# Turning an expert's inner rows in two row halves of the array instead of all at once

## The chip, the cores and the metric

The kernel runs on one core of a Trainium2 chip. The metric is the device time of one execution in microseconds (us), here the median of 3 runs. Engines are named as the profile names them: PE is TensorE's matmul, PEld its load of the stationary operand (the weights of a matmul), DVE is VectorE, ACT ScalarE, POOL GpSimd, SP SyncE, whose queue issues the loads from HBM.

## The reference

A decoder trunk of two layers on 256 tokens of width 1024, all in float32. Layer 0 is attention (dilated windows and differential heads) and a dense SwiGLU. Layer 1 is a gated linear recurrence and then eight SwiGLU experts, of which each token takes its two best:

```python
logits = (t @ w_router).astype(F32)
top_vals, top_idx = lax.top_k(logits, TOP_K)
top_w = jax.nn.softmax(top_vals, axis=-1)
gates = jnp.sum(jax.nn.one_hot(top_idx, N_EXPERTS, dtype=F32) * top_w[..., None], axis=1)
out = jnp.zeros((B * S, D), F32)
for e in range(N_EXPERTS):
    y = swiglu(t, w_gate[e], w_up[e], w_down[e]).astype(F32)
    out = out + gates[:, e:e + 1] * y
```

`swiglu(u, w_gate, w_up, w_down)` is `(silu(u @ w_gate) * (u @ w_up)) @ w_down`, with an inner width of 3584 per expert. The change touches the product in the outer brackets, the expert's inner rows, on its way from the up projection to the down projection.

## The kernel before

Experts are taken in pairs. The tokens of an expert are gathered into 128 slots by matmuls with one-hot matrices (`gather_steps`, L1121), so that the slots are the columns of `xgh` and `xgl`, the high and the low part of the activations. Each expert's inner width is cut into 7 chunks of 512; one expert and one chunk is a `Job` (L1187), 56 in all.

A job has four pieces. `gate` and `up` multiply the slots by 512 columns of two weights and leave 128 slots x 512 inner columns in PSUM; `up` multiplies the two on DVE into `hm` (L1227), with the slots on the partitions. The down projection needs the inner columns on the partitions, so `turn` (L1231) transposes `hm` in four blocks of 128x128 by TensorE (L1235) into one PSUM bank, from which ACT copies the high part `hh` (L1239) and DVE subtracts it to give the low part `hl` (L1240). `down` multiplies them by 512 rows of the third weight.

Weights come as raw float32 tiles by SP's queue (L85), 14 of them in a ring. Each piece of 128x1024 elements, a split, is divided on ACT into a high part `w_hi` and on DVE into a low part `w_lo` (L91). A split is read by six matmuls of 512 columns: `mm3` (L100) multiplies high by high, high by low and low by high (L101 to L103), twice. Four splits are in flight, since `w_hi` and `w_lo` have four buffers each and `run` (L1168) makes a split ready three splits ahead of its use.

The order of the work of three engines is written out by hand. `in_turn` (L1113) issues a step behind the last step of PE, ACT and DVE that is in `tails`. `order` (L1342) puts the steps of neighbouring jobs between each other: the gate of a job, the turn of the job before, the up projection, the down of the job before. Where a pair of experts ends, the turn stands between two halves of the next gather, and the slots of the next pair follow (`slot_rows`, L1091). After the last job, turn and down follow each other directly.

PSUM has 8 banks: 4 with the tag `acc`, 2 with `pj` (the outputs of down), 2 with `tp`. `bank("tp")` (L75) hands out the two `tp` banks in rotation, to `turn` and to `slot_rows` among others.

Of the kernel before, what the change touches and what calls it, by code (L numbers as in the profile page):

```python
# [9 lines left out]
F32R = mybir.dt.float32r  # L10
I32 = mybir.dt.int32
U32 = mybir.dt.uint32
AF = mybir.ActivationFunctionType
# [3 lines left out]
P = 128  # L17
# [17 lines left out]
def f32(ap):  # L35
    return ap.bitcast(F32)
# [3 lines left out]
def tile_trunk(  # L40
# [22 lines left out]
    nc = tc.nc  # L63
# [11 lines left out]
    def bank(tag, bufs=2):  # L75
        return psum.tile([P, 512], F32, name=tag, tag=tag, bufs=bufs)
# [135 lines left out]
    ident = const.tile([P, P], F32, name="ident")  # L212
# [90 lines left out]
    def norm_T(hgs, gain, acc, into=None):  # L303

        xh, xl = into or x_tiles()
        rs = []
        for t in range(NT):
            for c in range(2):
                nc.vector.tensor_add(h[t][:, HALF[c]], acc[t][c], h[t][:, HALF[c]])
                nc.vector.tensor_mul(hgs[t][:, HALF[c]], h[t][:, HALF[c]], gain[:, HALF[c]])  # L310
            r, pw = rms(t)
            rs.append(r)
            for c in range(2):
                to_T(hgs[t], xh, xl, t, 4 * c, 4 * c + 4)
        return xh, xl, rs, pw
# [45 lines left out]
    with tc.tile_pool(name="att", bufs=2) as att, tc.tile_pool(name="atc", bufs=1) as atc:  # L361
# [19 lines left out]
        for t in range(NT):  # L381
            r = atc.tile([P, 2], F32, name=f"r2{t}")
# [41 lines left out]
        class Group:  # L424
# [49 lines left out]
            def turn(self):  # L474
                self.qT = att.tile([P, 2, S], F32, name="qT", tag="qT", bufs=1)
                self.kT = att.tile([P, 2, S], F32, name="kT", tag="kT", bufs=1)
                gq, gk = (cols[:, 2:3], cols[:, 3:4]) if self.g == 3 else (cols[:, 0:1], cols[:, 1:2])
                for t in range(NT):
                    pt = bank("tp")
                    for i in range(4):  # L480
                        nc.tensor.transpose(out=pt[:, i * P:(i + 1) * P], in_=self.qk[t][:, i * P:(i + 1) * P], identity=ident)
                    ptv = pt.rearrange("p (a b) -> p a b", b=P)
                    nc.scalar.activation(self.qT[:, :, TOK[t]], ptv[:, 0:2], AF.Copy, scale=gq)
                    nc.vector.tensor_scalar(self.kT[:, :, TOK[t]], ptv[:, 2:4], gk, None, op0=ALU.mult)
# [227 lines left out]
    with tc.tile_pool(name="hga", bufs=2) as hga, tc.tile_pool(name="hg", bufs=2) as hg, tc.tile_pool(name="hgc", bufs=1) as hgc:  # L712
        C = 64
# [261 lines left out]
    moe = ctx.enter_context(tc.tile_pool(name="moe", bufs=2))  # L975
# [9 lines left out]
    _, _, rx, pw = norm_T(hg_, gain_m, acc, into=dense)  # L985
# [125 lines left out]
    tails = {}  # L1111

    @contextmanager  # L1113
    def in_turn():

        with ExitStack() as st:
            for i in tails.values():
                st.enter_context(tc.issue_after(i.ins))
            yield
# [67 lines left out]
    class Job:  # L1187
# [41 lines left out]
            return self.into(self.wu) + [out_]  # L1229

        def turn(self):  # L1231
            pt = bank("tp")
            with in_turn():
                for i in range(4):
                    tails["pe"] = nc.tensor.transpose(out=pt[:, i * P:(i + 1) * P], in_=self.hm[:, i * P:(i + 1) * P], identity=ident)  # L1235
                self.hh = moe.tile([P, 4, P], F32R, name="hh", tag="hh", bufs=1)
                self.hl = moe.tile([P, 4, P], F32R, name="hl", tag="hl", bufs=1)
                ptv = pt.rearrange("p (a b) -> p a b", b=P)
                tails["act"] = nc.scalar.activation(self.hh, ptv, AF.Copy)  # L1239
                tails["dve"] = nc.vector.tensor_sub(self.hl, ptv, f32(self.hh))  # L1240

        def down(self):
            sh, ch = self.shared, self.ch
# [145 lines left out]
    with tc.If(most > P):  # L1389
        ecur = mc.tile([P, 1], F32, name="ecur")  # L1390
        nc.vector.memset(ecur, 0.0)
        with tc.For_i(0, NE, 1) as e:
# [16 lines left out]
            for src, dst in ((nh, xg2[0]), (nl, xg2[1])):  # L1409
                for k0 in range(0, KT, 4):  # L1410
                    pt = bank("tp")
# [54 lines left out]
```

## Time and profile before

| | |
|---|---|
| median of 3 runs | 1479.27 us (1476.80 to 1481.37) |
| the profiled execution | 1475.87 us, of it a span of 1474.2 us from the first to the last instruction |
| mean granted TensorE clock over the span | 0.996 of full speed |
| busy PE, PEld, DVE, ACT | 1439.5, 1220.1, 1231.7 and 1059.0 us |
| the stretch of the experts | from about 500 us to the end |

Matmuls are pipelined: one starts before the one ahead of it has ended, so a busy time of PE is no measure of how well the array is used. The pace of PE is read from the distance between starts. PEld overlaps PE: the load of the next matmul's weights usually runs under the stream of the one before.

### The profile page before, as it was taken

Reading aid. Unit: us, or ns where it says so; the run is one execution under the profiler, and the core shown is the slowest. Engines: PE = TensorE matmul, PEld = TensorE weight load, DVE = VectorE, ACT = ScalarE, POOL = GpSimd, SP = SyncE. Lnnn points to the kernel's source line nnn. Section 1 sums busy time; section 2 is a strip of 40 time slices with the busy share of each in tenths; the row PEclk is TensorE's granted clock in tenths of the full one; section 3 lists DMA queues with packets and bytes.
Section 4 is the critical chain, followed back from the end, with each engine's and each line's share of the span. In section 5 each row is a group of like instructions: output and inputs, shape, how many; then the busy total and the mean of one; then the engine's idle time right before and its main releaser. Section 6 shows DMA issues by size and latency. Waiting matters only on the chain.

```text
span 1474.2 us, 20073 instructions
## 1 busy us (share of the span) xinstructions
PE 1439.5 (98%) x7509; PEld 1220.1 (83%) x7509; DVE 1231.7 (84%) x1460; ACT 1059.0 (72%) x1285; POOL 32.5 (2%) x45
## 2 busy tenths in 40 slices
PE   7999999999999999999999999999999999999996
PEld 6887899998889788888888888888888888888885
DVE  7776656556867899999999999989999999999995
ACT  6655544445756688888888888888888888888884
POOL 1000000000000100000000000000000000000000
PEclk9999999999999999999999999999999999999998
DMA  9933355656443399999999999999999999999971
GB/s 315 369 131 115 129 189 183 184 188 186 137 165 135 137 349 378 376 375 383 371 345 378 375 369 384 392 337 384 370 376 366 394 378 344 380 370 372 384 266 16
DMA packets 209692, 434.05 MB, mean 294 GB/s; under 512 B 7403, under 2 KB 58643, under 8 KB 209587
## 3 DMA queue, kind: packets, MB, share of 16 engines
q1 hardware_dynamic: 207506, 425.77, 79.8%
q0 software_dynamic: 2080, 6.92, 2.1%
q8 instruction: 61, 1.00, 0.3%
q14 instruction: 45, 0.36, 0.1%
HBM read 427.41 MB, written 5.24 MB: 293 GB/s over the span
## 4 chain that ended last, share of the span: by engine, by line
issue 61%; PE 29%; DMA 5%; DVE 2%; ACT 2%; POOL 0%; SPq 0%; POOLq 0%; ACTq 0%; DVEq 0%
DMA out_dram<-y,idx 4%; PE acc L101 3%; PE acc L102 3%; PE acc L103 3%; PE pj L342 3%; PE pj L344 3%; PE pj L343 3%; PE pj L101 1%; PE pj L103 1%; PE pj L102 1%; PE pj L760 1%; PE pj L761 1%; PE pj L762 1%; DVE w_lo L91 1%; PE tp L556 1%
## 5 line engine op out<-in xcount | busy, mean ns | idle before, releaser
L91 DVE TENSOR_TENSOR w_lo<-raw,w_hi 128x1024 fp32r<-128x1024 f32 x810 | 975.1, 1223 | 156.6 <-ACT w_hi L91 116.9
L91 ACT ACTIVATE w_hi<-raw 128x1024 fp32r<-128x1024 f32 x810 | 853.5, 1062 | 299.7 <-PE acc L103 127.5
L101 PE MATMUL acc<-w_hi,xgh 128*128 128x512 f32 x904 | 357.2, 395 | 0.9 <-ACT xgh L294 0.9
L103 PE MATMUL acc<-w_hi,xgl 128*128 128x512 f32 x904 | 352.7, 390 | 0.0
L102 PE MATMUL acc<-w_lo,xgh 128*128 128x512 f32 x904 | 352.4, 390 | 0.0
L103 PEld LDWEIGHTS acc<-w_hi,xgl 128*128 128x128 f32 x904 | 169.7, 188 | 36.1
L101 PEld LDWEIGHTS acc<-w_hi,xgh 128*128 128x128 f32 x904 | 169.8, 188 | 34.9 <-ACT xgh L294 1.2
L102 PEld LDWEIGHTS acc<-w_lo,xgh 128*128 128x128 f32 x904 | 169.9, 188 | 33.6
L103 PE MATMUL pj<-w_hi,hl 128*128 128x512 f32 x448 | 174.5, 389 | 0.0
L102 PE MATMUL pj<-w_lo,hh 128*128 128x512 f32 x448 | 174.3, 389 | 0.0
L101 PE MATMUL pj<-w_hi,hh 128*128 128x512 f32 x448 | 163.5, 390 | 0.7 <-ACT hh L1239 0.7
L101 PEld LDWEIGHTS pj<-w_hi,hh 128*128 128x128 f32 x448 | 84.1, 188 | 18.2 <-ACT hh L1239 0.9
L103 PEld LDWEIGHTS pj<-w_hi,hl 128*128 128x128 f32 x448 | 84.1, 188 | 17.9 <-DVE hl L1240 0.4
L102 PEld LDWEIGHTS pj<-w_lo,hh 128*128 128x128 f32 x448 | 84.1, 188 | 17.4
L342 PE MATMUL pj<-xh,w_hi 128*128 128x256 f32 x320 | 90.8, 284 | 0.6 <-DVE hm L677 0.6
L344 PE MATMUL pj<-xh,w_lo 128*128 128x256 f32 x320 | 90.6, 283 | 0.0
L343 PE MATMUL pj<-xl,w_hi 128*128 128x256 f32 x320 | 90.6, 283 | 0.0
L342 PEld LDWEIGHTS pj<-xh,w_hi 128*128 128x128 f32 x320 | 61.4, 192 | 1.2 <-DVE hm L677 0.8
L343 PEld LDWEIGHTS pj<-xl,w_hi 128*128 128x128 f32 x320 | 61.4, 192 | 0.4
L344 PEld LDWEIGHTS pj<-xh,w_lo 128*128 128x128 f32 x320 | 61.4, 192 | 0.0
L101 PE MATMUL acc<-w_hi,xh 128*128 128x512 f32 (+1 forms) x160 | 58.7, 368 | 1.5 <-ACT xh L294 0.8
L102 PE MATMUL acc<-w_lo,xh 128*128 128x512 f32 (+1 forms) x160 | 57.6, 361 | 0.0
(300 smaller groups left out, 1538.5 us busy)
## 6 DMA issues: line engine op xcount, KB each, us to landing
raw<-in_moe_w_gate_dram SPq DMA_DIRECT2D x112, 1024.0 KB, 7.5
raw<-in_moe_w_up_dram SPq DMA_DIRECT2D x112, 1024.0 KB, 7.7
raw<-in_moe_w_down_dram SPq DMA_DIRECT2D x110, 1024.0 KB, 7.3
raw<-in_ffn_w_gate_dram SPq DMA_DIRECT2D x22, 512.0 KB, 3.7
raw<-in_ffn_w_up_dram SPq DMA_DIRECT2D x22, 512.0 KB, 4.8
raw<-in_ffn_w_down_dram SPq DMA_DIRECT2D x11, 1024.0 KB, 4.9
raw<-in_hgrn_w_in_dram SPq DMA_DIRECT2D x10, 1024.0 KB, 5.6
raw<-in_attn_w_in_dram SPq DMA_DIRECT2D x16, 512.0 KB, 8.9
```

The lines of the kernel that those rows point to most:

```text
L91: split.last = nc.scalar.activation(hi, view, AF.Copy), nc.vector.tensor_sub(lo, view, f32(hi))
L101: nc.tensor.matmul(ps, lhsT=xh, rhs=wh, start=first, stop=False, skip_group_check=chk)
L102: nc.tensor.matmul(ps, lhsT=xh, rhs=wl, start=False, stop=False, skip_group_check=chk)
L103: return nc.tensor.matmul(ps, lhsT=xl, rhs=wh, start=False, stop=last, skip_group_check=chk)
L342: nc.tensor.matmul(o, lhsT=wh[:, i, j], rhs=xh[:, k], start=k == 0 and j == 0, stop=False, skip_group_check=True)
L343: nc.tensor.matmul(o, lhsT=wh[:, i, j], rhs=xl[:, k], start=False, stop=False, skip_group_check=True)
L344: nc.tensor.matmul(o, lhsT=wl[:, i, j], rhs=xh[:, k], start=False, stop=k == KT - 1, skip_group_check=True)
L556: nc.tensor.matmul(po[:, j * 64:(j + 1) * 64], lhsT=pT[:, kb, j, :], rhs=v[:, kb, j * 64:(j + 1) * 64], start=(j == 0 and kb == 0), stop=( ...
L760: nc.tensor.matmul(o, lhsT=wh[:, k], rhs=xh[:, k], start=first, stop=False, skip_group_check=True)
L761: nc.tensor.matmul(o, lhsT=wh[:, k], rhs=xl[:, k], start=False, stop=False, skip_group_check=True)
L762: nc.tensor.matmul(o, lhsT=wl[:, k], rhs=xh[:, k], start=False, stop=last, skip_group_check=True)
```

## The change

`turn` transposes the slots in two halves, partitions 0 to 63 and 64 to 127. Each of the four blocks becomes two transposes with 64 rows of `hm` as stationary operand and a 64x64 corner of the identity as moving operand, in alternation between the halves. The first half's results go into one `tp` bank and the second half's into the other, 256 columns each. ACT and DVE make `hh` and `hl` from the two banks in two instructions each. C is 64.

```diff
         def turn(self):
-            pt = bank("tp")
+            pts = [bank("tp") for _ in range(2)]
+            self.hh = moe.tile([P, 4, P], F32R, name="hh", tag="hh", bufs=1)
+            self.hl = moe.tile([P, 4, P], F32R, name="hl", tag="hl", bufs=1)
+            parts = [slice(r * C, (r + 1) * C) for r in range(2)]
             with in_turn():
+
                 for i in range(4):
-                    tails["pe"] = nc.tensor.transpose(out=pt[:, i * P:(i + 1) * P], in_=self.hm[:, i * P:(i + 1) * P], identity=ident)
-                self.hh = moe.tile([P, 4, P], F32R, name="hh", tag="hh", bufs=1)
-                self.hl = moe.tile([P, 4, P], F32R, name="hl", tag="hl", bufs=1)
-                ptv = pt.rearrange("p (a b) -> p a b", b=P)
-                tails["act"] = nc.scalar.activation(self.hh, ptv, AF.Copy)
-                tails["dve"] = nc.vector.tensor_sub(self.hl, ptv, f32(self.hh))
+                    for rr, pt in zip(parts, pts):
+                        m = nc.tensor.transpose(out=pt[:, i * C:(i + 1) * C], in_=self.hm[rr, i * P:(i + 1) * P], identity=ident[rr, rr])
+                tails["pe"] = m
+                for rr, pt in zip(parts, pts):
+                    ptv = pt[:, 0:4 * C].rearrange("p (a b) -> p a b", b=C)
+                    a = nc.scalar.activation(self.hh[:, :, rr], ptv, AF.Copy)
+                    d = nc.vector.tensor_sub(self.hl[:, :, rr], ptv, f32(self.hh[:, :, rr]))
+                tails["act"], tails["dve"] = a, d
```

## Rows read from the trace of the kernel before

**Rows 1.** The page, busy us, share of the span and instructions of each engine.
```profile
PE 1439.5 (98%) x7509; PEld 1220.1 (83%) x7509; DVE 1231.7 (84%) x1460; ACT 1059.0 (72%) x1285; POOL 32.5 (2%) x45
```

**Rows 2.** Busy us per stretch: PE, PEld, DVE, ACT, POOL, then clock, DMA share, GB/s.
```profile
800.00:1100.00 300.00, 300.00 (x1374) 249.09 (x1373) 278.27 (x256) 243.78 (x254) 3.64 (x2) 1.00 1.01 374
```

**Rows 3.** Groups, 525 to 1456 us: count | busy us, mean ns | idle before, releasers.
```profile
L91 DVE TENSOR_TENSOR w_lo<-raw,w_hi 128x1024 fp32r<-128x1024 f32 x656 | 787.2, 1223 | 57.6 <-ACT w_hi L91 20.1
...
L1240 DVE TENSOR_TENSOR hl<-tp,hh 128x512 fp32r<-128x512 f32 x55 | 38.0, 692 | 9.2 <-ACT hh L1239 9.0
...
L1235 PE MATMUL tp<-ident,hm 128*128 128x128 f32 x218 | 32.7, 272 | 0.0
L1239 ACT ACTIVATE hh<-tp 128x512 fp32r<-128x512 f32 x55 | 32.6, 592 | 0.9 <-PE tp L1235 0.9
L1235 PEld LDWEIGHTS tp<-ident,hm 128*128 128x128 f32 x217 | 26.9, 140 | 6.7
```

**Rows 4.** Timeline around one turn: start us, us, engine, line, what, count.
```profile
915.12 0.40 PE L103 MATMUL acc<-w_hi,xgl 128*128 128x512 f32 x1
...
915.36 0.60 PE L1235 MATMUL tp<-ident,hm 128*128 128x128 f32 x4
...
915.80 0.19 PEld L102 LDWEIGHTS acc<-w_lo,xgh 128*128 128x128 f32 x1
```

**Rows 5.** Timeline, layer 0's attention scores, row halves alternating into two banks.
```profile
62.86 0.39 PE L103 MATMUL acc<-w_hi,xl 128*128 128x512 f32 x1
63.17 0.52 PEld L510 LDWEIGHTS pj<-kT,qT 64*128 64x128 f32 x8 [0.35 <-issue]
63.18 0.71 PE L510 MATMUL pj<-kT,qT 64*128 64x128 f32 x8
...
63.82 0.19 PEld L101 LDWEIGHTS acc<-w_hi,xh 128*128 128x128 f32 x1
...
63.93 0.19 PEld L102 LDWEIGHTS acc<-w_lo,xh 128*128 128x128 f32 x1
```

**Rows 6.** Timeline, layer 1's recurrence, matmuls on 64 rows of the array.
```profile
385.19 1.42 PEld L877 LDWEIGHTS tp<-v,kt 64*128 64x128 f32 x12
385.19 1.61 PE L877 MATMUL tp<-v,kt 64*128 64x128 f32 x12
...
386.73 0.19 PEld L760 LDWEIGHTS pj<-xh,w_hi 128*128 128x128 f32 x1
```

**Rows 7.** Timeline, the router's transposes of 8 rows.
```profile
497.00 0.39 PE L101 MATMUL acc<-w_hi,xgh 128*128 128x512 f32 x1
...
497.32 0.20 PEld L1036 LDWEIGHTS tp<-ident,lT 8*128 8x128 f32 x2 [0.36 <-DVE lT L1033]
```

**Rows 8.** Groups, 100 to 125 us: the same two copies at half the size.
```profile
L294 DVE TENSOR_TENSOR xl<-tp,xh 128x256 fp32r<-128x256 f32 x2 | 0.8, 416 | 0.0
...
L294 ACT ACTIVATE xh<-tp 128x256 fp32r<-128x256 f32 x2 | 0.8, 390 | 0.0
```

**Rows 9.** Timeline behind the turn of rows 4.
```profile
917.62 3.50 DVE L91 TENSOR_TENSOR w_lo<-raw,w_hi 128x1024 fp32r<-128x1024 f32 x3 [0.26 <-ACT w_hi L91]
...
919.91 0.19 PEld L102 LDWEIGHTS acc<-w_lo,xgh 128*128 128x128 f32 x1
```

**Rows 10.** Timeline of PE where a pair of experts ends.
```profile
979.03 0.60 PE L1235 MATMUL tp<-ident,hm 128*128 128x128 f32 x4
979.38 0.59 PE L1096 MATMUL tp<-info,oneh 128*128 128x4 f32 x4
```

**Rows 11.** Timeline, turn and down of the last job.
```profile
1456.16 0.60 PE L1235 MATMUL tp<-ident,hm 128*128 128x128 f32 x4
1456.79 0.60 ACT L1239 ACTIVATE hh<-tp 128x512 fp32r<-128x512 f32 x1 [0.74 <-PE tp L1235]
...
1457.44 0.19 PEld L101 LDWEIGHTS pj<-w_hi,hh 128*128 128x128 f32 x1 [0.92 <-ACT hh L1239]
...
1458.16 0.19 PEld L103 LDWEIGHTS pj<-w_hi,hl 128*128 128x128 f32 x1 [0.43 <-DVE hl L1240]
```

## The prediction

> **What bounds the kernel now.** The page's first part comes first: PE is busy for 98% of the span [rows 1]. Since matmuls overlap, that alone proves little. The stretches follow: in 300 us of the experts' part PE has no hole, the granted clock is 1.00 (the level of 2.4 GHz), DVE works 278 us and ACT 244 us, and HBM delivers 374 GB/s [rows 2]. The groups of the same part then say who waits: the idle time ahead of PE's transposes is 0.0, while DVE and ACT wait for each other and for PE [rows 3]. So PE sets the pace between 525 and 1456 us, and DVE is next with 93%. What the array does in a turn is worth its full length there; what ACT and DVE do is worth nothing until they are late.
>
> The timeline of one turn gives its price [rows 4]. The last matmul of the gate starts at 915.12. Four transposes start from 915.36 on; they take 0.60 us together and the last 0.27 [rows 3], which puts starts 0.11 us apart. The first matmul behind them begins to stream when the load of the one after it begins, at 915.80. From last matmul to next matmul: 0.68 us. Nothing is drained: the loads run under the streams ahead of them.
>
> **The change part by part.** The number of columns that stream stays: 4 transposes of 128 become 8 of 64. A gain needs two halves of the array to work at the same time, and the trace shows that they can. In layer 0, eight matmul instructions on 64 rows each, in alternation between the halves and into two banks, have their loads in 0.52 us [rows 5]; one takes 0.19, so first and last start 0.33 apart. That is three intervals of 0.11, so the eight went as four pairs. Twelve such loads that did not pair, in the recurrence, took 1.42 us, 0.11 apart each [rows 6].
>
> The same block shows what it costs to get in and out. The last full matmul starts at 62.86 and the first load on half the rows at 63.17: 0.31 us, where a successor in full rows starts after 0.23 (72 matmuls and a turn of 0.45 fill a job's 16.8 us). The 0.09 between is a drain, and the load behind it is covered by nothing. At the other end the last pair starts at 63.18 + 0.71 - 0.27 = 63.62, streams 0.11, and the next load is at 63.82: another 0.09. That load, too, is open, until 63.93. The recurrence has the same exit: 385.19 + 1.61 - 0.27 = 386.53 to 386.73, 0.20 [rows 6]. The router's transposes of 8 rows enter 0.32 after the start of the matmul ahead [rows 7].
>
> So the turn after the change, from the start of the gate's last matmul to the start of the next one:
>
> - to the first load: 0.31 [rows 5].
> - the first load, open: 0.06. A load for a transpose is shorter than for a matmul: 140 ns against 190 as recorded [rows 3, 5], and two of them with 8 rows took 0.20 together, so they start 0.06 apart [rows 7].
> - three intervals between four pairs: 64 columns at 0.11 per 128 make 0.055, the load 0.06; the longer one counts, 0.17 in all.
> - the last pair's start to the next load: 0.20 less the half of 0.11, as 64 columns stream and not 128: 0.15.
> - the next load, open: 0.11 [rows 5].
>
> The sum is 0.80 us against 0.68: 0.12 us more per turn. In words: pairing saves some 0.2 us of streaming, and two drains with two open loads cost 0.33.
>
> No row has transposes in alternating halves, so the bounds: at worst a block costs as much as that of rows 5, which streams twice the columns: 63.93 - 62.86 = 1.07, or 0.39 more per turn. At best pairs cost no drain: 0.68 - 0.22 = 0.46, or 0.22 less. I take 0.12, since entry, exit and pairing each have rows of their own, and only the halving of the width is worked out.
>
> The Trainium skill, "TensorE: Matmul & The Clock Gate", section "LDWEIGHTS (loading the stationary operand)", has a load take its columns divided by 1.2 GHz whatever the rows, here 107 ns. By that the first load and the three intervals would be 0.11 each, and the sum an estimated 1.01 us, 0.33 more per turn. The 0.06 between two loads of 128 columns speaks against it for transposes.
>
> ACT makes two copies of 390 ns in place of one of 592, DVE two of 416 in place of one of 692 [rows 3, 8]: 0.19 and 0.14 us more per turn. Queued behind them are the next `w_hi` on ACT and `w_lo` on DVE, and PE waits for that. The tightest place is the fourth split behind a turn: its `w_lo` starts at 917.62, ends 1.22 later at 918.84, and its first reader loads at 919.91 [rows 9]. Of 1.07 us some 0.33 go at most, and the reader is 0.12 later. Over a job DVE then works 12 x 1.223 + 0.83 + 0.69 = 16.2 us of 16.9 and still catches up. Price: nothing. If that cover were gone, 0.33 us per turn, 18 us in all.
>
> Two banks are now taken per turn, of two. The turn before is a job away, so `turn` itself waits for nothing. At the end of a pair of experts, though, `slot_rows` follows the transposes directly [rows 10] and needs the first of these banks, which is free once ACT and DVE have finished the first half, 0.39 + 0.42 us and some waiting later. Sixteen gather matmuls stand ready to go first. I take 0; three stalls of 1.1 us, 3 us, if not.
>
> In the last job nothing covers the turn: PE waits for `hh` and then for `hl` [rows 11]. There the drains run under a wait, and the halves let DVE start on the first while ACT copies the second: 0.39 + 2 x 0.42 = 1.23 us plus hand-overs against 0.59 + 0.69 = 1.28. I take 0 for this one.
>
> DMA issues are not moved. Sum: 55 turns x 0.12 = 6.6 us. On the profiled execution's own time, 1475.87, that makes 1482.5. This execution lies 3.4 us below the median of the three runs, 1479.27, and the forecast for a median is 1486 us, 0.45% slower. About 0.3%, 4.4 us, is what a measurement of this kernel can tell from no change.
>
> **The rivals.**
>
> *The halves do not pair.* The recurrence's matmuls on half rows alternate in the code and still ran one after the other [rows 6]; the order on the engine is not always the order in the code. Then eight intervals of 0.06 take the place of four: 0.31 + 0.06 + 7 x 0.06 + 0.15 + 0.11 = 1.05, so 0.37 more per turn, 20 us, 1499. The same comes out, near enough, if they pair but each load takes 0.11 (18 to 19 us), or if the copies eat the slack. Against it: both banks are free at every turn, so nothing reorders the halves.
>
> *Faster: full and half rows change over without a drain when both are transposes or the queue is full.* The place is the start of the first load after the gate: if it comes 0.01 after the array is free, as in the turn of before [rows 4], and not 0.09, and the loads hide, then 0.68 - 0.22 per turn, 55 x 0.22 = 12 us less, 1467. It decides from the point at which entry and exit together cost under 0.2 us. Against it stand the changes of rows in three parts of the trace [rows 5, 6, 7].
> The Trainium skill, "TensorEngine Tiling (Array Packing)", section "Theoretical Speedup", promises up to 2x for a small dimension of 64, which is this case; the same page names the drain on a change of mode but gives it no price.
>
> *No change that can be told.* If half of the open loads or drains hides, the turn costs under 0.08 us more, which is within 4.4 us. For it speaks that PE's queue is full here, whereas the blocks of rows 5 and 7 had waited for DVE or ACT shortly before.
>
> **How the numbers follow.** The forecast, 4 to 9 us slower, 0.62; no pairing, slow loads or late copies, 15 to 22 us slower, 0.20; no change, 0.12; faster, 0.06. Some of the forecast's own range lies at the bound, so slower has 0.80, same 0.14 and faster 0.06. The range reaches from the better end of the forecast, 1482, to the case without pairing, 1499; 1482 to 1489 is the likeliest case's own.
>
> **What would show it.** The transposes should come as pairs that start within 0.01 us, four starts 0.06 apart, in a block of 64-row instructions like that of rows 5. The gate's last matmul to the first load should be 0.31 us, the last pair to the next load 0.15, and the distance from one turn to the next 0.12 longer than the 16.8 of before. PE should still wait for nobody. The prediction is wrong if the first load comes less than 0.25 after the gate's last matmul, if eight starts stand apart, or if PE waits for `w_lo` or a bank.

## The result, and the profile after

The changed kernel takes 1485.6 us in the median, the kernel before 1476.8 in the runs beside it: a ratio of 1.0063, with a 95% interval of 1.0051 to 1.0075. It is slower by 9.3 us by the ratio and by 8.8 by the medians, and by more than 0.3%. One of its seven executions, at a granted clock of 0.805, took 1691.94 us and is left out of the ratio. The profiled execution has a span of 1483.8 us against 1474.2.

The page's first part and the stretch of rows 2, in the changed kernel; PE still has no hole, and clock and HBM are as before:

```profile
PE 1447.8 (98%) x7733; PEld 1212.3 (82%) x7733; DVE 1235.5 (83%) x1516; ACT 1062.0 (72%) x1341; POOL 32.5 (2%) x45
```
```profile
800.00:1100.00 300.00, 300.00 (x1436) 244.32 (x1435) 276.39 (x272) 242.86 (x272) 3.64 (x2) 1.00 1.00 370
```

The timeline of one turn, which answers to [rows 4]:

```profile
542.93 0.39 PE L103 MATMUL acc<-w_hi,xgl 128*128 128x512 f32 x1
...
543.25 0.33 PEld L1240 LDWEIGHTS tp<-ident,hm 64*128 64x128 f32 x8 [0.35 <-issue]
543.25 0.46 PE L1240 MATMUL tp<-ident,hm 64*128 64x64 f32 x8
...
543.64 0.19 PEld L101 LDWEIGHTS acc<-w_hi,xgh 128*128 128x128 f32 x1
...
543.75 0.19 PEld L102 LDWEIGHTS acc<-w_lo,xgh 128*128 128x128 f32 x1
543.85 0.66 ACT L1244 ACTIVATE hh<-tp 128x256 fp32r<-128x256 f32 x2
...
544.26 0.76 DVE L1245 TENSOR_TENSOR hl<-tp,hh 128x256 fp32r<-128x256 f32 x2
```

From the gate's last matmul to the first matmul behind the turn: 543.75 - 542.93 = 0.82 us, where it was 0.68. The first load comes 0.32 after that matmul. Eight loads take 0.33 together; one takes 0.14 (below), so the first and the last start 0.19 apart, in three steps of 0.06. A window that ends behind the second pair shows the pairs: four loads in 0.20, which is one step of 0.06 and one load of 0.14.

```profile
543.25 0.20 PEld L1240 LDWEIGHTS tp<-ident,hm 64*128 64x128 f32 x4 [0.35 <-issue]
```

The groups from 526.5 to 1463 us (count | busy us, mean ns | idle us before), which answer to [rows 3]:

```profile
L91 DVE TENSOR_TENSOR w_lo<-raw,w_hi 128x1024 fp32r<-128x1024 f32 x654 | 787.8, 1224 | 70.9 <-ACT w_hi L91 31.5
...
L1245 DVE TENSOR_TENSOR hl<-tp,hh 128x256 fp32r<-128x256 f32 x110 | 41.6, 420 | 0.3
...
L1244 ACT ACTIVATE hh<-tp 128x256 fp32r<-128x256 f32 x110 | 36.1, 385 | 0.8 <-PE tp L1240 0.8
...
L1240 PE MATMUL tp<-ident,hm 64*128 64x64 f32 x440 | 25.4, 235 | 0.0
L1240 PEld LDWEIGHTS tp<-ident,hm 64*128 64x128 f32 x436 | 17.7, 137 | 18.4 <-issue 18.0
```

The last line shows the way in: PEld has 18.4 us of idle time ahead of the transposes' loads, put down to "issue", the name for time in which nothing that the profile shows is waited for. In the kernel before it was 6.7 [rows 3]. The 11.7 between them is not itself the loss, which was 8.1 and is read from the distances below. The transposes' union of busy time went the other way, from 32.7 us to 25.4: the pairs do save. A reader who ranks lines by busy time would take the change for a gain.

The turns are now 16.95 us apart, by 0.15 more than before, and 55 x 0.147 (0.817 - 0.670, before rounding) makes 8.1 us; from the first turn to the last it took 939.77 us, and 931.56 before. The spans differ by 9.6; most of the rest came ahead of any changed instruction, for the first turn starts at 526.30 in this execution and at 524.59 in the one of before.

### The profile page after: what moved, and what is told of

It is laid out like the page before. It is cut to its first block, busy times and chain, and to the rows that moved or that the text cites. A ratio compares the mean times of both kernels' runs of the same rounds, so it can differ in the third digit from the quotient of the medians.

```text
span 1483.8 us, 20633 instructions
## 1 busy us (share of the span) xinstructions
PE 1447.8 (98%) x7733; PEld 1212.3 (82%) x7733; DVE 1235.5 (83%) x1516; ACT 1062.0 (72%) x1341; POOL 32.5 (2%) x45
## 4 chain that ended last, share of the span: by engine, by line
PE 87%; issue 7%; ACT 2%; DVE 2%; DMA 1%; POOL 0%; SPq 0%; POOLq 0%; ACTq 0%; DVEq 0%
PE acc L101 16%; PE acc L102 16%; PE acc L103 16%; PE pj L101 7%; PE pj L102 7%; PE pj L103 7%; PE pj L342 3%; PE pj L344 3%; PE pj L343 3%; PE tp L1240 1%; PE acc L1133 1%; PE pj L760 1%; PE pj L761 1%; DVE w_lo L91 1%; PE pj L762 1%
## 5 line engine op out<-in xcount | busy, mean ns | idle before, releaser
L103 PEld LDWEIGHTS pj<-w_hi,hl 128*128 128x128 f32 x448 | 84.1, 188 | 17.7 <-DVE hl L1245 0.3
```

The costliest lines, as they stand in the source:

```text
L103: return nc.tensor.matmul(ps, lhsT=xl, rhs=wh, start=False, stop=last, skip_group_check=chk)
```

## The experiments

Times are medians beside runs of the kernel before on the same chip: 1477.4 us for `control`, `full_two_banks`, `one_half_row` and `halves_in_a_row`, 1477.0 for the four kernels with 8 or 16 blocks in the table below, 1477.7 for `one_side` and `halves_x4_in_a_row`.

**The kernel before once more** (`control`, no edit). 

> The kernel before, unchanged. The changed kernel's first turn started 1.9 us later than before's, ahead of any changed instruction. If that is chance from execution to execution, this profile may start its first turn anywhere between 523 and 528 us and has turns 16.80 us apart; if the change moves something ahead of the first turn, it starts at 524.4 us again.

Measured: 1476.95 us; the first turn starts at 525.62.

```profile
525.62 0.60 PE L1235 MATMUL tp<-ident,hm 128*128 128x128 f32 x4
```

The same program began its first turn 1.0 us later than in the profile before, and with the other kernels' profiles, whose first turns lie between 524.5 and 529.9, that makes the start a matter of the execution. The part of the difference that belongs to the change is in the turns.

**The banks and the copies alone** (`full_two_banks`).

```diff
-            pt = bank("tp")
+            pts = [bank("tp") for _ in range(2)]
...
-                    tails["pe"] = nc.tensor.transpose(out=pt[:, i * P:(i + 1) * P], in_=self.hm[:, i * P:(i + 1) * P], identity=ident)
+                    tails["pe"] = nc.tensor.transpose(out=pts[i // 2][:, i % 2 * P:(i % 2 + 1) * P],
+                                                      in_=self.hm[:, i * P:(i + 1) * P], identity=ident)
...
+                for n, pt in enumerate(pts):
+                    ptv, ab = pt[:, 0:2 * P].rearrange("p (a b) -> p a b", b=P), slice(2 * n, 2 * n + 2)
+                    tails["act"] = nc.scalar.activation(self.hh[:, ab], ptv, AF.Copy)
+                    tails["dve"] = nc.vector.tensor_sub(self.hl[:, ab], ptv, f32(self.hh[:, ab]))
```

> The kernel before with its four full transposes, but two into each of two banks, and with two copies of half the size on ACT and on DVE: the change without the row halves. Theory of drains: the copies are covered by 1.07 us of slack, so within 3 us of before, 1477 us. Rival, that the copies or the second bank cost what was lost: 0.15 us per turn, 8 us, 1485 us.

Measured: 1476.7 us, a ratio of 0.9995 (0.9984 to 1.0006). Two banks and twice the copies cost nothing that can be told: from the first turn to the last this kernel took 931.58 us, the kernel before 931.56. What was lost was lost on PE.

**One narrow transpose more** (`one_half_row`), in the kernel before.

```diff
-            pt = bank("tp")
+            pt, extra = bank("tp"), bank("tp")
...
+                tails["pe"] = nc.tensor.transpose(out=extra[:, 0:64], in_=self.hm[0:64, 0:P], identity=ident[0:64, 0:64])
```

> The kernel before with one more transpose per turn, 64 rows wide, behind the four full ones, into a bank that nobody reads. Theory of drains: from the start of the last full transpose 0.11 us of stream, 0.09 of drain, 0.06 of open load, 0.05 of stream, 0.09 of drain and 0.11 of open load, 0.51 us in place of 0.11, so 0.40 us more per turn, 22 us, 1499 us. Rival, that a change of rows costs little and the eight instructions cost what was lost: the stream of one narrow transpose, 0.06 us per turn, 3 us, 1480 us.

Measured: 1501.9 us, a ratio of 1.0161 (1.0144 to 1.0178), 24 us. The timeline of its loads (PEld), and then that of PE, around one turn:

```profile
613.42 0.59 PEld L1235 LDWEIGHTS tp<-ident,hm 128*128 128x128 f32 x4
614.18 0.14 PEld L1236 LDWEIGHTS tp<-ident,hm 64*128 64x128 f32 x1 [0.17 <-issue]
614.39 0.19 PEld L101 LDWEIGHTS acc<-w_hi,xgh 128*128 128x128 f32 x1
614.50 0.19 PEld L102 LDWEIGHTS acc<-w_lo,xgh 128*128 128x128 f32 x1
```
```profile
613.42 0.40 PE L103 MATMUL acc<-w_hi,xgl 128*128 128x512 f32 x1
613.65 0.60 PE L1235 MATMUL tp<-ident,hm 128*128 128x128 f32 x4
```

From 613.42 to 614.50 it is 1.08 us, 0.40 more than the turn before, for one instruction that streams 64 columns. The last full transpose starts at 613.65 + 0.60 - 0.27 = 613.98 and streams 0.11; the narrow one's load comes at 614.18, 0.09 after that. The way into half rows and out again is paid in full by a single instruction. It is the same between two transposes as between matmul and transpose. A wait for a semaphore is not behind it: the narrow transpose waits for none. The first full transpose here waits for the same one as the first narrow transpose of the changed kernel, and yet its load comes at 613.42, right behind the start of the matmul ahead.

**No pairs by force** (`one_side`): all eight transposes on rows 0 to 63, so that the second half of the slots gets the first half's rows.

```diff
-                        m = nc.tensor.transpose(out=pt[:, i * C:(i + 1) * C], in_=self.hm[rr, i * P:(i + 1) * P], identity=ident[rr, rr])
+                        m = nc.tensor.transpose(out=pt[:, i * C:(i + 1) * C], in_=self.hm[0:C, i * P:(i + 1) * P], identity=ident[0:C, 0:C])
```

> The changed kernel, but all eight transposes of a turn on rows 0 to 63, into the two banks as before: the second half of the slots gets the first half's rows. Nothing can pair, whatever the engine looks ahead. Theory of drains and pairs: seven intervals of 0.0615 us in place of three, 0.25 us more per turn than the changed kernel, 14 us, 1499 us. Rival, that pairing saves nothing and starts of pairs are only how the trace shows them: 1485 us.

Measured: 1497.9 us, a ratio of 1.0133 (1.0108 to 1.0158), 12 us above the changed kernel, by medians of two sets of runs. Timeline of one turn:

```profile
610.94 0.39 PE L103 MATMUL acc<-w_hi,xgl 128*128 128x512 f32 x1
...
611.26 0.57 PEld L1240 LDWEIGHTS tp<-ident,hm 64*128 64x128 f32 x8 [0.35 <-issue]
...
611.90 0.19 PEld L101 LDWEIGHTS acc<-w_hi,xgh 128*128 128x128 f32 x1
```

Eight loads now take 0.57 us, seven steps of 0.06, where the changed kernel had three. Entry and exit are the same: 0.32 to the first load, and 0.15 from the last stream's start to the next load. Pairing is real, and against the same eight without pairs it saves 0.25 us per turn.

**One half behind the other** (`halves_in_a_row`).

```diff
-                for i in range(4):
-                    for rr, pt in zip(parts, pts):
+                for rr, pt in zip(parts, pts):
+                    for i in range(4):
```

> The changed kernel, but all four transposes of the first half, then all four of the second. Theory of pairs and drains: neighbours are on the same rows and cannot pair, so seven intervals of 0.06 us replace three plus the offset of a pair, 0.25 us more per turn than in the changed kernel, 14 us, 1499 us. Rival, that the price of the change is in its eight instructions and not in their order: 1486 us, as the changed kernel.

Measured: 1484.6 us, a ratio of 1.0048 (1.0033 to 1.0062), as the changed kernel. My expectation was wrong here. The rival had the number but not the reason: the price is not one of eight instructions as such, since eight on one side cost 12 us more (`one_side`). Timeline of one turn:

```profile
610.43 0.39 PE L103 MATMUL acc<-w_hi,xgl 128*128 128x512 f32 x1
...
610.75 0.33 PEld L1240 LDWEIGHTS tp<-ident,hm 64*128 64x128 f32 x8 [0.35 <-issue]
...
611.15 0.19 PEld L101 LDWEIGHTS acc<-w_hi,xgh 128*128 128x128 f32 x1
...
611.26 0.19 PEld L102 LDWEIGHTS acc<-w_lo,xgh 128*128 128x128 f32 x1
```

Eight loads in 0.33 us again: three steps. The four of the second half stand behind all four of the first, in the code and in the order of PE's instructions as the program is built, and still run beside them. So in blocks of four the alternation in the code gives nothing; the engine makes the pairs itself, if it finds work for the free rows soon enough.

**How soon is soon enough** (`halves_x4_in_a_row`): each block transposed four times, so that 16 of one half stand ahead of 16 of the other.

```diff
-                for i in range(4):
-                    for rr, pt in zip(parts, pts):
+                for rr, pt in zip(parts, pts):
+                    for i in 4 * list(range(4)):
```

> The changed kernel with each block transposed four times, first the 16 of one half and then the 16 of the other. With 4 and 4 the second half ran under the first, though it came behind it in the queue. If the engine looks ahead over 16 transposes too, 1526 us, as with alternating halves. If it looks ahead over fewer, part of the second half comes alone: wholly alone would be 16 more intervals of 0.0615 us, 0.98 us per turn, 54 us, 1580 us; in between by as many as are out of its reach.

Measured: 1571.2 us, a ratio of 1.0635 (1.0605 to 1.0665). Its loads around one turn, and below them those of the same 32 transposes in alternation (`halves_x4`, next):

```profile
600.07 1.87 PEld L1240 LDWEIGHTS tp<-ident,hm 64*128 64x128 f32 x32 [0.35 <-issue]
602.01 0.19 PEld L101 LDWEIGHTS acc<-w_hi,xgh 128*128 128x128 f32 x1
602.12 0.19 PEld L102 LDWEIGHTS acc<-w_lo,xgh 128*128 128x128 f32 x1
```
```profile
613.97 1.07 PEld L1240 LDWEIGHTS tp<-ident,hm 64*128 64x128 f32 x32 [0.35 <-issue]
615.11 0.19 PEld L101 LDWEIGHTS acc<-w_hi,xgh 128*128 128x128 f32 x1
615.22 0.19 PEld L102 LDWEIGHTS acc<-w_lo,xgh 128*128 128x128 f32 x1
```

The one has (1.87 - 0.14) / 0.062 = 28 steps, the other 15. With 31 steps for no pair at all, three of 16 met. Here, too, the built program has all 16 of one half ahead of the 16 of the other. In every turn the second half's first load is the 14th to start, beside the 14th of the first half; in the turn shown it starts at 600.87, and the semaphore that it asks for was last raised at 600.16, so that no wait held it back. So the second half starts when three transposes of the first are still to come. In `halves_in_a_row` it starts 0.01 us after the first one, when three are to come as well: in blocks of four the order does not matter because four is within that reach.

**More blocks per stretch** (`full_x2`, `full_x4` from the kernel before; `halves_x2`, `halves_x4` from the changed one): each block transposed twice or four times into the same place.

```diff
-                for i in range(4):
+                for i in 2 * list(range(4)):
```

> The kernel before with each block transposed twice, so that a turn has 8 full transposes. Both theories: 4 more at 0.109 us each per turn, 0.43 us, 56 turns, 24 us, 1501 us.

> The changed kernel with each block transposed twice, so that a turn has 8 pairs in one stretch of half rows. Theory of drains, which are paid once per stretch: 4 more pairs at 0.0615 us, 0.25 us per turn, 14 us, 1499 us, about 2 us below the full rows with twice the blocks. Rival, that each narrow transpose carries the loss with it: twice the distance between changed kernel and before, 1518 us.

> The kernel before with each block transposed four times, 16 full transposes per turn. Both theories: 12 more at 0.109 us, 1.30 us per turn, 73 us, 1550 us.

> The changed kernel with each block transposed four times, 16 pairs in one stretch. Theory of drains: 12 more pairs at 0.0615 us, 0.74 us per turn, 41 us, 1527 us, some 23 us below the full rows with four times the blocks: the same edit with the other sign. Rival, that each narrow transpose carries the loss: four times the distance, 1585 us.

The ratios are to the kernel before in the runs beside each.

| blocks per turn | full rows, us (ratio) | half rows, us (ratio) | half less full, us |
|---|---|---|---|
| 4 | 1476.8 | 1485.6 (1.0063) | +8.8 |
| 8 | 1503.9 (1.0171, 1.0153 to 1.0190) | 1499.3 (1.0149, 1.0131 to 1.0168) | -4.6, intervals overlap |
| 16 | 1547.7 (1.0476, 1.0458 to 1.0493) | 1525.9 (1.0329, 1.0312 to 1.0346) | -21.8 |

The same edit turns from a loss into a gain as the stretch grows. At eight blocks the medians cannot tell the two apart; by the traces a turn takes 1.106 us in full rows and 1.067 in half rows, 0.04 less, 2 us in 55 turns. Timeline of PE, then of PEld, around one turn of 16 blocks in full rows:

```profile
617.20 0.39 PE L103 MATMUL acc<-w_hi,xgl 128*128 128x512 f32 x1
617.44 1.91 PE L1235 MATMUL tp<-ident,hm 128*128 128x128 f32 x16
```
```profile
619.07 0.19 PEld L101 LDWEIGHTS acc<-w_hi,xgh 128*128 128x128 f32 x1
619.18 0.19 PEld L102 LDWEIGHTS acc<-w_lo,xgh 128*128 128x128 f32 x1
```

and around one in half rows, timeline of PE; the loads behind it are shown above:

```profile
613.65 0.39 PE L103 MATMUL acc<-w_hi,xgl 128*128 128x512 f32 x1
613.97 1.21 PE L1240 MATMUL tp<-ident,hm 64*128 64x64 f32 x32
```

Full rows take 619.18 - 617.20 = 1.98 us, half rows 615.22 - 613.65 = 1.57. The 0.41 between them, 55 times, is 22.5 us, against 21.8 between the medians. A block costs 0.109 in full rows and 0.0615 as a pair, 0.047 less, and the stretch costs 0.33 once; they meet at seven blocks.

That gives a version of this kernel: two jobs' turns in one stretch of eight blocks. By these numbers it would save 0.05 us per two turns, 1.4 us in all. That is below what a measurement can tell, it needs `hm`, `hh` and `hl` twice, and it was not run.

## Why the prediction was right

**PE sets the pace, and the turn counts in full.** Right. The turns moved apart by as much as the turn on PE grew, 0.15 us, and PE waits for nobody between 526 and 1463 us.

**Pairs save 0.2 us per turn.** Right in kind and size: four blocks at 0.047 less than in full rows make 0.19 us. Against half rows without pairs it is 0.25 (`one_side`).

**Two drains and two open loads cost 0.33.** Right. The terms were 0.31, 0.06, 0.17, 0.15 and 0.11; the trace, whose records are in ns, has 0.317, 0.059, 0.184, 0.150 and 0.108, and the two starts of a pair are 3 to 4 ns apart. `one_half_row` shows the price without any pairs: 0.40, of which 0.06 is the narrow transpose's own step.

**0.12 us per turn.** The mis-sized term: it is 0.147. Nothing was left out. Both sums, 0.80 and 0.68, were put together from rows rounded to 0.01, and the small difference between them took the whole of the error: the first was 0.82, the second 0.67. The largest part is a slip in the three intervals, which were put at 0.17 although three loads of 0.06 make 0.18; they took 0.184. Over 55 turns that is 1.5 us: 8.1 where 6.6 was forecast. The medians differ by 8.8, and the 0.7 that remains is within the spread of the start that `control` shows. That the forecast of 1486 us and the median of 1485.6 agree to 0.4 is partly luck: the forecast set out from 1479.27, and the kernel before took 1476.8 in the runs beside the changed one, so a start 2.5 us too high hid an addition 2.2 too small.

**The load of a transpose at 0.06 and not 0.11.** Right: the steps are 0.06 in every kernel with half rows. Where the Trainium skill's "TensorE: Matmul & The Clock Gate", section "LDWEIGHTS (loading the stationary operand)", has a load take its columns divided by 1.2 GHz, the trace disagrees for transposes, and agrees for the matmul behind them, whose open load takes 0.108.

**ACT and DVE cost nothing.** Right: `full_two_banks` has a ratio of 0.9995, with the copies at 386 and 419 ns, as in the changed kernel (385 and 420).

**`slot_rows` waits for a bank, at no price.** Right, and by the way that was named. Timeline of PE where a pair of experts ends, which answers to [rows 10]: the gather's second half now goes first, and L1096 comes 2.6 us after the turn. The distances between turns grew by as much there as everywhere else, 0.14 to 0.16 us.

```profile
984.76 0.46 PE L1240 MATMUL tp<-ident,hm 64*128 64x64 f32 x8
985.15 0.74 PE L1133 MATMUL acc<-oneh,nh 128*128 128x256 f32 x4
...
987.16 0.39 PE L101 MATMUL pj<-w_hi,hh 128*128 128x512 f32 x1
987.39 0.50 PE L1096 MATMUL tp<-info,oneh 128*128 128x4 f32 x4
```

**The last turn costs nothing.** Right: from its first transpose to the end of the span it is 17.7 us, and 18.0 before. Timeline, which answers to [rows 11]:

```profile
1466.06 0.33 PEld L1240 LDWEIGHTS tp<-ident,hm 64*128 64x128 f32 x8 [0.35 <-issue]
...
1467.27 0.19 PEld L101 LDWEIGHTS pj<-w_hi,hh 128*128 128x128 f32 x1 [0.88 <-ACT hh L1244]
...
1467.86 0.19 PEld L103 LDWEIGHTS pj<-w_hi,hl 128*128 128x128 f32 x1 [0.29 <-DVE hl L1245]
```

**The rivals.** That the halves do not pair had its price right, 1499 forecast and 1498 in `one_side`, but its reason wrong. I took the recurrence's unpaired block [rows 6] for a matter of order. `halves_in_a_row` shows that order alone within four does not keep halves apart. Timeline of DVE at that block in the kernel before:

```profile
385.30 0.74 DVE L867 COPY_PREDICATED st<-mki,tp 128x512 f32<-128x512 int32 x1 [0.68 <-PE tp L864]
```

The second half's bank is freed by this copy, at 386.04, and by then the eight loads of the first half were all but done (385.19 + 8 x 0.11 = 386.07). The second half's first matmul waits for the semaphore that this copy raises, and its load starts at 386.09. In the built program the two halves do not alternate here as they do in the code, but stand one behind the other. Later in the same kernel, where they do alternate and the bank was free, the same line took 0.96 us for its twelve loads:

```profile
418.74 0.96 PEld L877 LDWEIGHTS tp<-v,kt 64*128 64x128 f32 x12
```

There eight loads went as four pairs, and the four behind them, all on one half, alone. So at 385 the bank kept the halves apart. At every turn of the changed kernel both banks were free, as the prediction had it against this rival.

The faster rival falls on the way in and out: the first load came 0.317 us after the gate's last matmul in the changed kernel, and 0.32 in every kernel whose turn begins on half rows. With 16 blocks in a stretch the gain is 1.98 to 1.57 us, 1.26x. A block within the stretch gains more, 0.109 to 0.0615 us, 1.77x. The Trainium skill's "TensorEngine Tiling (Array Packing)", section "Theoretical Speedup", has up to 2x for this case, and the same page names the drain without a price; the trace shows the price, and no run reached 2x.

## What to carry to other kernels

A stretch of half rows has a fixed price, here 0.33 us for the way in and out, and a saving per pair, here 0.047 us for a 128x128 block in float32: count the blocks per stretch first, since four lost, eight came out about even and sixteen won. The price can be read in the kernel at hand wherever a matmul with few rows stands between full ones, from the start of the full one ahead to the second load behind. Where PE sets the pace, read the distance between the neighbours' starts and not the busy time of the edited line: that of the transposes on PE fell here by 7 us while the kernel lost 9.

## What the runs showed of the hardware

The second half of the rows does not wait for its turn in the queue. Four transposes on rows 64 to 127 that stood behind four on rows 0 to 63 ran beside them, at the same 0.33 us for eight loads as in alternation. Since the built program has them in this order, it is the engine that let them overtake. The look ahead is short: of 16 behind 16, three met, in every turn.
